# A decoder layer with the residual kept unscaled, one GpSimd instruction a norm, GpSimd's subtractions in quarters and a later load of x

## The chip, the cores and the metric

The kernel runs on one core of one Trainium2 chip. The metric is the device time of one execution in microseconds (us), the median of several runs. The engines that matter are TensorE (PE: matmuls, with its weight loads as PEld), VectorE (DVE), ScalarE (ACT), GpSimd (POOL), and the queue of SyncE (SP) that issues nearly all transfers.

## The reference

One decoder layer over 512 positions with 1024 features, all in 32-bit floats:

```
x = layer_norm(ALPHA * x + 0.5 * swiglu(x, ffn1...), ln1)        # first FFN, inner width 2816
q, f, i, g, conv_val, conv_gate = split(x @ w_in)
o_a = rms_norm(gated linear recurrence of q, f, i) * gain * sigmoid(g)      # 4 heads of 128
o_b = silu(layer_norm(causal conv of width 31 of conv_val * sigmoid(conv_gate)))
x = layer_norm(ALPHA * x + concat(o_a, o_b) @ w_out, ln2)
x = layer_norm(ALPHA * x + 0.5 * swiglu(x, ffn2...), ln3)        # second FFN
```

Here swiglu(x) is (silu(x @ w_gate) * (x @ w_up)) @ w_down, ALPHA is the fourth root of 2, layer_norm subtracts the mean, multiplies with (variance + epsilon) to the power of -1/2, and applies gain and bias. Multiplying the whole input of a layer norm by a constant changes nothing if its epsilon is multiplied by the constant's square.

## The kernel before

Every float32 product is made of three matmuls over operands that are split in two parts: `hi` is a rounded copy (`cast`, on ACT), and `lo` is what is left (`rest`, a subtraction raw - hi, L71). For weights the subtraction is on DVE or, for 22 units of 128x1024 that the middle part of the layer uses, on POOL (`plan(..., nc.gpsimd)`). The names in the trace are `raw` for loaded weights, `whi` and `wlo` for their parts, `h`, `hp`, `ah`, `al`, `xh`, `xl` for activations and their parts, `bank` for PSUM banks.

The order of the program is: a start, in which x and the first weights are loaded and split; the first FFN's gate and up products, in which most pairs of blocks use seven products in place of eight (L405); its down product in `rows_out`; the mix (projections by `cols` and `rows`, the recurrence's `scores`, the convolution on DVE at L759, its norm); the output projection, in `rows_out` again; and the second FFN like the first. TensorE's order is written out by hand (`manual_schedule`), and the instructions of the other engines are put in order by the framework's scheduler; each engine works through its own in that order. A weight load can start when a buffer of `raw` is free, a cast when one of six slots for parts is.

The residual stream lies in four tiles `xres`, one for each 128 positions. `rows_out` computes its product in two halves of 512 features. After the second half of tile i it does the following on DVE and POOL:

- `add` (L328, L329): xres = product * factor + xres on DVE, and the half's statistics.
- `norm` (L334 to L342): the statistics are joined (L334); `rstd_of` computes (variance * scale + epsilon) to the power of -1/2 with two POOL instructions of one element a partition (L216, L217); meanwhile DVE does (xres - mean) * gain in two halves (L338); then, once `rstd` is there, xres * rstd + bias in two halves (L342).
- `finish(i)`, later in PE's order: PE transposes the normed tile (L269 after the first FFN, L283 after the mix), ACT and DVE split the transposed tile (L272, L273; L285 to L287), and POOL multiplies the tile by ALPHA for the next residual sum (`scaled`, L292). After the second FFN the tile is stored instead.

So that PE has work while a tile is being normed, `follow` puts the first products of the next stage between the transposes of the last tiles, by the fixed counts in `NORM_WAITS`.

`scaled` is also called for x itself: `load_rest` (L638) loads the four tiles of x into `xres` and scales them; the text of the program calls it in the first FFN, ahead of its third pair of blocks. `rstd_of` also serves the convolution's norm (L865, one element a partition, four times) and the recurrence's norm (8 elements, twice).

Of the kernel before, what the change touches and what calls it, by code (L numbers as in the profile page):

```python
# [9 lines left out]
F32 = mybir.dt.float32  # L10
# [43 lines left out]
def decoder_layer(ctx, tc, x_tok, x_q, w_first, vec, bcast, ng, w_gu1, w_d1, w_i, w_g, w_col, w_o, w_gu2, w_d2, out):  # L54
# [13 lines left out]
        nc.scalar.copy(hi, raw)  # L68

    def rest(lo, raw, hi, engine=nc.vector):  # L70
        engine.tensor_tensor(lo, raw, hi.bitcast(F32), op=ALU.subtract)  # L71

    def split(raw, hi, lo, lo_engine):
        cast(hi, raw)
# [136 lines left out]
        for j in range(2):  # L211
            nc.sync.dma_start(out=t[:, j, :], in_=bcast[2 * i + j:2 * i + j + 1, :].broadcast_to([P, D]))

    def rstd_of(square, scale, eps, n):
        r = small.tile([P, n], F32, tag=f"rstd{n}", name="rstd")
        nc.gpsimd.tensor_scalar(r, square, scale, eps, op0=ALU.mult, op1=ALU.add)  # L216
        nc.gpsimd.tensor_tensor(r, r, negh.broadcast_to([P, n]) if n > 1 else negh, op=ALU.pow)  # L217
        return r

# [68 lines left out]
        if i == NT - 1:  # L288
            x.sums()

    def scaled(i):
        nc.gpsimd.tensor_scalar(xres[i], xres[i], ALPHA, 1.0, op0=ALU.mult, op1=ALU.mult)  # L292


    def run(steps):
        for _ in steps:
# [14 lines left out]
    def rows_out(ks, per, lhs, accs, factor, late, finish, follow=(), before=lambda u: None, then=lambda: None):  # L311

        n_units = len(ks) // per
        stats = [small.tile([P, 2, 6], F32, tag="stats", name="stats") for _ in range(NT)]

        def part(acc, u, hi, lo, i):
            for j in range(per):  # L320
                n = per * u + j
                h, l = lhs(ks[n])
                mm3(acc[i], h[:, i * P:(i + 1) * P], l[:, i * P:(i + 1) * P],
                    hi[:, j, :], lo[:, j, :], n == 0, n == len(ks) - 1)

        def add(acc, half, i):
            z = xres[i][:, half * 512:(half + 1) * 512]
            nc.vector.scalar_tensor_tensor(z, acc[i], factor, z, op0=ALU.mult, op1=ALU.add)  # L328
            nc.vector.bn_stats(stats[i][:, half, :], z)  # L329

        def norm(i):
            gain, bias = gb
            mv = small.tile([P, 2], F32, tag="mv", name="mv")
            nc.vector.bn_aggr(mv, stats[i])  # L334
            r = rstd_of(mv[:, 1:2], 1.0, LN_EPS, 1)
            for c in range(2):
                s = slice(c * 512, (c + 1) * 512)
                nc.vector.scalar_tensor_tensor(xres[i][:, s], xres[i][:, s], mv[:, 0:1], gain[:, s],  # L338
                                               op0=ALU.subtract, op1=ALU.mult)
            for c in range(2):  # L340
                s = slice(c * 512, (c + 1) * 512)
                nc.vector.scalar_tensor_tensor(xres[i][:, s], xres[i][:, s], r, bias[:, s],  # L342
                                               op0=ALU.mult, op1=ALU.add)

        acc = [bank(b) for b in accs[0]]
        with tc.manual_schedule(engines={PE}):
            for u in range(n_units):
                before(u)
                hi, lo = unit()
                for i in range(NT):  # L350
                    part(acc, u, hi, lo, i)
        for i in range(NT):
            add(acc, 0, i)
        acc = [bank(b) for b in accs[1]]
        for u in range(n_units - late):
            hi, lo = unit()
            for i in range(NT):
                part(acc, u, hi, lo, i)
        then()
        ahead(late)  # L360
        kept = [(u, *unit_now()) for u in range(n_units - late, n_units)]
        ahead(SLOTS - late)
        with tc.manual_schedule(engines={PE}):
            left = deque()
            for i in range(NT):
                for n, (u, hi, lo) in enumerate(kept):
                    part(acc, u, hi, lo, i)
                    if n == 0 and i >= 2 and left:
                        left.popleft()()
                if i == NT - 1:  # L370
                    ahead(SLOTS)
                add(acc, 1, i)
                norm(i)
                left.append(finish(i))
            follow = iter(follow)
            for wait in NORM_WAITS:
                while wait > 0.0 and (t := next(follow, None)) is not None:
                    wait -= t
                left.popleft()()
            run(follow)  # L380

    def four_halved(pp, banks):

        ahead(4)
        us = [unit_now() for _ in range(4)]
        xh, xl = operand
        pp.extend(bank(b) for b in banks)
        for t in range(2):
            sl = slice(256 * t, 256 * (t + 1))
            for ps, (hi, lo) in zip(pp, us):  # L390
                for k in range(NK):
                    mm3(ps[:, sl], hi[:, k, :], lo[:, k, :], xh[:, k, sl], xl[:, k, sl], k == 0, k == NK - 1)
                    yield MM3 / 2
        ahead(AHEAD)
# [70 lines left out]
                    yield MM3 / 2  # L465
        ahead(AHEAD)

    def ffn(x, begun, meanwhile, gb_i, finish, follow=(), then=lambda: None, later=lambda: None):
        with tc.tile_pool(name="ffn", bufs=1) as fp:

            slots = ["h2", "h3", "v", "c", "h4", "h5"]
# [31 lines left out]
            with tc.manual_schedule(engines={PE}):  # L503
                plain_gate_up(begun)
                for f in range(1, PLAIN):
                    ahead(4)
                    ws = [unit_now() for _ in range(2)]
                    ahead(3)
                    got = [bank(i, 2, H) for i in chain(*zip(*PAIR_BANKS[f % 2]))]
                    run(plain(got, x, ws))  # L510
                    plain_gate_up(got)
                for f in range(PLAIN, NP):
                    if f == PLAIN:
                        meanwhile()
                    h.append(h_of(f))
                    for s in range(2):
                        ahead(3)
                        w = unit_now()
                        ahead(3)
                        pr = Pair(PAIR_BANKS[f % 2][s], work_tile() if s else h[f])  # L520
                        for n in USUAL:
                            run(pr.steps(x, w, (n,)))
                            if f == PLAIN and s == 0 and n == "p7":
                                x.last_sum()
                        gate_up(s, pr)
# [35 lines left out]
                f, l = divmod(n, 2)  # L561
                return tuple(y[:, l * T:(l + 1) * T] for y in hp[f])

            rows_out(range(NF), 2, lhs, FFN_ACCS, 0.5, 4, finish, follow, before, then)


    x1 = Halves()
# [67 lines left out]
            nc.gpsimd.tensor_copy(masks[:, n, :], mf)  # L635
        nc.gpsimd.tensor_copy(masks[:, len(MASKED), :], ident)

    def load_rest():  # L638
        for i in range(NT):
            nc.sync.dma_start(out=xres[i], in_=x_tok[i])  # L640
            scaled(i)

    def after(transpose, b):
        def finish(i):
            def rest():
                transpose(i, b)
                scaled(i)
            return rest
        return finish

    def lazily(make, *args):
# [4 lines left out]
    def next_operand(make):  # L656
        operand[:] = make()

    ffn(x1, begun, load_rest, 0, after(transposed, 4), four_halved(conv_first, (6, 7, 0, 1)),
        lambda: next_operand(plain_operand), make_masks)  # L660
    xh, xl = operand


    with tc.tile_pool(name="mix", bufs=1) as mp:
# [162 lines left out]
        def values(hp):  # L827
            for h in range(2):
                ps = bank(nbank[h][0], NT, P)
                for i in range(NT):  # L830
                    for j in range(i + 1):
                        s = diag[h][:, i, :] if i == j else off[h][:, at[j, i] * P:(at[j, i] + 1) * P]
                        nc.tensor.matmul(ps[:, i, :], lhsT=s, rhs=v[:, j, (2 * hp + h) * P:(2 * hp + h + 1) * P],  # L833
                                         start=(j == 0), stop=(j == i))
                nc.scalar.copy(ot[:, :, 2 * hp + h, :], ps)
                sq = small.tile([P, NT, P], F32, tag="work", name="sq", bufs=2)
                nc.scalar.activation(sq, ps, AF.Square)
                nc.vector.tensor_reduce(ss[:, 2 * hp + h, :], sq, axis=mybir.AxisListType.X, op=ALU.add)

        def norm_gate(hp, b):  # L840

            r = rstd_of(ss[:, 2 * hp:2 * hp + 2, :].rearrange("p a b -> p (a b)"), 1.0 / P, RMS_EPS, 2 * NT)
            for h in range(2):
                n = 2 * hp + h
                for i in range(NT):
# [9 lines left out]
        def conv_norm():  # L855

            def forth(i):
# [4 lines left out]
                nc.vector.bn_stats(stt, ps.rearrange("p a b -> p (a b)"))  # L862
                mv = small.tile([P, 2], F32, tag="mv", name="mv")
                nc.vector.bn_aggr(mv, stt)
                r = rstd_of(mv[:, 1:2], 1.0, LN_EPS, 1)  # L865
                cn = small.tile([P, 4, P], F32, tag="work", name="cn", bufs=2)
                nc.vector.tensor_scalar(cn, ps, mv[:, 0:1], r, op0=ALU.subtract, op1=ALU.mult)
                return cn
# [58 lines left out]
        def gates_between(u):  # L927
# [3 lines left out]
            elif u == 3:  # L931
# [2 lines left out]
        begun = []  # L934
        rows_out((4, 5, 6, 7, 0, 1, 2, 3), 2,
                 lambda k: (ah[:, k, :], al[k]) if k < NH else (bh[:, k - NH, :], bl[k - NH]),
                 ((2, 3, 6, 7), (0, 1, 4, 5)), 1.0, 4, after(transposed_halves, 6),
                 lazily(lambda: begin(begun, operand[0], (2, 3, 0, 1))),
                 before=gates_between, then=lambda: next_operand(lambda: [Halves()]))

# [3 lines left out]
            nc.sync.dma_start(out=out[i * P:(i + 1) * P, s], in_=xres[i][:, s])  # L944
        return lambda: None

    ffn(operand[0], begun, lambda: None, 2, store)


# [58 lines left out]
```

## Time and profile before

| | |
|---|---|
| time, median of 3 runs | 946.73 us (946.48 to 947.9) |
| the profiled execution, its own time | 949.64 us |
| its span from first to last instruction | 947.9 us |
| busy: PE, DVE, ACT, POOL | 932.6, 692.7, 388.6, 132.3 us |
| transfers | 96.67 MB, 102 GB/s in the mean |

The span is some 1.7 us shorter than the execution's own time, and this execution took 2.9 us longer than the median. Busy time is the time in which an engine works on an instruction; PE's matmuls overlap, and their ends are modelled, so its busy time holds some time in which it waits for its pipeline.

### The profile page before, as it was taken

The page shows a single profiled execution, that of the slowest core. Times are in us where ns is not written, and L with a number is a line of the kernel's source. Part 1 is how long each engine was busy: PE and PEld are TensorE (multiplying, and loading weights), DVE is VectorE, ACT ScalarE, POOL GpSimd, SP SyncE. Part 2 cuts the span into 40 slices and gives each one's busy share as a digit, 9 for nine tenths or more (in the row PEclk, how much of TensorE's full clock was granted, in tenths as well). Part 3 has the DMA queues.
Part 4 walks back from the last instruction along what each step waited for, and adds up shares of the span by engine and source line. Part 5 has one row for each costly group of instructions (what it writes and reads, how often), then busy time and mean ns, then how long its engine had stood idle before and what let it go on. Part 6 is the DMA issues. An engine that isn't in the chain of part 4 may idle for free.

```text
span 947.9 us, 14234 instructions
## 1 busy us (share of the span) xinstructions
PE 932.6 (98%) x5913; PEld 843.8 (89%) x5913; DVE 692.7 (73%) x915; ACT 388.6 (41%) x560; POOL 132.3 (14%) x106
## 2 busy tenths in 40 slices
PE   9999999999999999999999999999999999999996
PEld 6799999999888889888888888989999999988885
DVE  6988888887624276999887658958888888742417
ACT  5554555556421123414341723534555545722100
POOL 1100000000910035532352204100000000000002
PEclk9999999999999999999999999999999999999998
DMA  8432322324423303321130251223223222452302
GB/s 295 155 131 90 134 90 97 127 68 145 156 89 92 108 22 101 124 88 45 51 123 5 63 166 44 87 85 123 101 92 132 90 90 90 133 156 90 99 13 89
DMA packets 22464, 96.67 MB, mean 102 GB/s; under 512 B 2496, under 2 KB 3648, under 8 KB 17024
## 3 DMA queue, kind: packets, MB, share of 16 engines
q1 hardware_dynamic: 22320, 95.50, 30.1%
q8 instruction: 46, 0.75, 0.3%
q0 software_dynamic: 80, 0.26, 0.1%
q14 instruction: 18, 0.15, 0.1%
HBM read 93.66 MB, written 2.10 MB: 101 GB/s over the span
## 4 chain that ended last, share of the span: by engine, by line
PE 48%; DVE 3%; POOL 1%; issue 0%; POOLq 0%; DVEq 0%; ACT 0%
PE bank L405 19%; PE bank L191 9%; PE bank L189 9%; PE bank L190 9%; PE bank L776 1%; PE bank L833 1%; DVE wlo L71 1%; DVE xres L342 0%; POOL rstd L217 0%; DVE al L286 0%; PE bank L799 0%; POOL rstd L216 0%; DVE qk L808 0%; DVE diag L816 0%; DVE stats L329 0%
## 5 line engine op out<-in xcount | busy, mean ns | idle before, releaser
L71 DVE TENSOR_TENSOR wlo<-raw,whi 128x1024 fp32r<-128x1024 f32 (+2 forms) x150 | 175.1, 1175 | 146.6 <-ACT whi L68 146.5
L68 ACT CAST whi<-raw 128x1024 fp32r<-128x1024 f32 (+2 forms) x172 | 173.4, 1013 | 254.8 <-PE bank L191 151.8
L189 PE MATMUL bank<-whi,hp 128*128 128x512 f32 x320 | 124.7, 390 | 0.0
L191 PE MATMUL bank<-whi,hp 128*128 128x512 f32 x320 | 124.5, 389 | 0.0
L190 PE MATMUL bank<-wlo,hp 128*128 128x512 f32 x320 | 124.5, 389 | 0.0
L405 PE MATMUL bank<-ah,whi 128*128 128x256 f32 x432 | 122.3, 283 | 0.0
L405 PE MATMUL bank<-bh,whi 128*128 128x256 f32 x432 | 122.3, 283 | 0.0
L405 PE MATMUL bank<-bl,whi 128*128 128x256 f32 x432 | 122.3, 283 | 0.0
L405 PE MATMUL bank<-ah,wlo 128*128 128x256 f32 x432 | 122.2, 283 | 0.0
L405 PE MATMUL bank<-al,whi 128*128 128x256 f32 x432 | 122.2, 283 | 0.0
L405 PE MATMUL bank<-bh,wlo 128*128 128x256 f32 x432 | 122.1, 283 | 0.0
L405 PEld LDWEIGHTS bank<-bh,whi 128*128 128x128 f32 x432 | 82.9, 192 | 0.0
L405 PEld LDWEIGHTS bank<-bl,whi 128*128 128x128 f32 x432 | 82.9, 192 | 0.0
L405 PEld LDWEIGHTS bank<-bh,wlo 128*128 128x128 f32 x432 | 82.9, 192 | 0.0
L405 PEld LDWEIGHTS bank<-al,whi 128*128 128x128 f32 x432 | 82.9, 192 | 0.1
L405 PEld LDWEIGHTS bank<-ah,whi 128*128 128x128 f32 x432 | 82.8, 192 | 0.1
L405 PEld LDWEIGHTS bank<-ah,wlo 128*128 128x128 f32 x432 | 82.8, 192 | 0.0
L759 DVE SCALAR_TENSOR_TENSOR bank<-u,vecs,bank 128x512 f32<-128x512 f32 x120 | 81.2, 751 | 1.8 <-ACT bank L754 1.6
L216 POOL TENSOR_SCALAR rstd<-mv 128x1 f32<-128x1 f32 x16 | 8.7, 542 | 466.9 <-DVE mv L334 451.7
L191 PEld LDWEIGHTS bank<-whi,hp 128*128 128x128 f32 x320 | 60.1, 188 | 12.5
L190 PEld LDWEIGHTS bank<-wlo,hp 128*128 128x128 f32 x320 | 60.1, 188 | 12.5
L189 PEld LDWEIGHTS bank<-whi,hp 128*128 128x128 f32 x320 | 60.1, 188 | 12.2
(193 smaller groups left out, 1963.1 us busy)
## 6 DMA issues: line engine op xcount, KB each, us to landing
raw<-w_gu SPq DMA_DIRECT2D x42, 1024.0 KB, 4.8
raw<-w_d SPq DMA_DIRECT2D x44, 512.0 KB, 3.5
raw<-w_col SPq DMA_DIRECT2D x16, 512.0 KB, 3.5
raw<-w_o SPq DMA_DIRECT2D x8, 512.0 KB, 3.4
xres<-x_tok SPq DMA_DIRECT2D x4, 512.0 KB, 7.8
gb<-bcast SPq DMA_DIRECT2D x4, 512.0 KB, 4.7
raw<-w_i SPq DMA_DIRECT2D x4, 512.0 KB, 3.4
raw<-w_g SPq DMA_DIRECT2D x4, 512.0 KB, 3.4
```

The source lines that it names most:

```text
L68: nc.scalar.copy(hi, raw)
L71: engine.tensor_tensor(lo, raw, hi.bitcast(F32), op=ALU.subtract)
L189: nc.tensor.matmul(ps, lhsT=lh, rhs=rh, start=first, stop=False)
L190: nc.tensor.matmul(ps, lhsT=lh, rhs=rl, start=False, stop=False)
L191: nc.tensor.matmul(ps, lhsT=ll, rhs=rh, start=False, stop=last)
L216: nc.gpsimd.tensor_scalar(r, square, scale, eps, op0=ALU.mult, op1=ALU.add)
L405: nc.tensor.matmul(ps, lhsT=l[:, k, :], rhs=r[:, k, :], start=first and k == 0 and j == 0, stop=k == 3 and j == 2, skip_group_check=True)
L759: nc.vector.scalar_tensor_tensor(accs[n], us[n][:, j:j + T], vecs[:, w:w + 1], accs[n], op0=ALU.mult, op1=ALU.add)
L776: nc.tensor.matmul(ps[:, g, :], lhsT=k[:, h, sl], rhs=q[:, h, sl], start=True, stop=True)
L833: nc.tensor.matmul(ps[:, i, :], lhsT=s, rhs=v[:, j, (2 * hp + h) * P:(2 * hp + h + 1) * P], start=(j == 0), stop=(j == i))
```

## The change

- `xres` holds the normed tile itself and not ALPHA times it. The products are added with the factor divided by ALPHA (0.5 / ALPHA or 1 / ALPHA), and the norms over this sum use epsilon / ALPHA squared. The 12 POOL instructions of `scaled` (128x1024 each) are gone.
- `rstd_of` has one POOL instruction: the epsilon is added by a DVE instruction, and the recurrence's mean over 128 features is made by a scale in ACT's squaring, which was there before. There are 18 such norms.
- A subtraction on POOL is issued as four instructions of a quarter of the columns (128x256). Those on DVE stay whole.
- The text of the program loads x later: after `make_masks`, in the first FFN's down product.

```diff
     def rest(lo, raw, hi, engine=nc.vector):
-        engine.tensor_tensor(lo, raw, hi.bitcast(F32), op=ALU.subtract)
+
+        n = raw.shape[-1]
+        step = n // 4 if engine is nc.gpsimd else n
+        for j in range(0, n, step):
+            sl = slice(j, j + step)
+            engine.tensor_tensor(lo[..., sl], raw[..., sl], hi.bitcast(F32)[..., sl], op=ALU.subtract)
...
-    def rstd_of(square, scale, eps, n):
+    def rstd_of(square, eps, n):
         r = small.tile([P, n], F32, tag=f"rstd{n}", name="rstd")
-        nc.gpsimd.tensor_scalar(r, square, scale, eps, op0=ALU.mult, op1=ALU.add)
+        nc.vector.tensor_scalar(r, square, eps, None, op0=ALU.add)
         nc.gpsimd.tensor_tensor(r, r, negh.broadcast_to([P, n]) if n > 1 else negh, op=ALU.pow)
...
-    def scaled(i):
-        nc.gpsimd.tensor_scalar(xres[i], xres[i], ALPHA, 1.0, op0=ALU.mult, op1=ALU.mult)
...
-            r = rstd_of(mv[:, 1:2], 1.0, LN_EPS, 1)
+            r = rstd_of(mv[:, 1:2], LN_EPS / ALPHA ** 2, 1)
...
-                    if f == PLAIN:
-                        meanwhile()
...
-            rows_out(range(NF), 2, lhs, FFN_ACCS, 0.5, 4, finish, follow, before, then)
+            rows_out(range(NF), 2, lhs, FFN_ACCS, 0.5 / ALPHA, 4, finish, follow, before, then)
...
-    def load_rest():
+    def later():
+        make_masks()
         for i in range(NT):
             nc.sync.dma_start(out=xres[i], in_=x_tok[i])
-            scaled(i)
...
-            def rest():
-                transpose(i, b)
-                scaled(i)
-            return rest
+            return lambda: transpose(i, b)
...
-                nc.scalar.activation(sq, ps, AF.Square)
+                nc.scalar.activation(sq, ps, AF.Square, scale=P ** -0.5)
```

The first place is SyncE's queue near the start of the program. These are its rows before; `vec` is a small table, `x_tok` is x by tiles, `w_gu` the first FFN's weights and `w_d` those of its down product:

```order
L603 DMA vecs<-vec 128x144
L640 DMA xres_73<-x_tok 128x1024
L640 DMA xres_74<-x_tok 128x1024
L98 DMA raw<-w_gu 128x2048 x2
L640 DMA xres_75<-x_tok 128x1024
L640 DMA xres_76<-x_tok 128x1024
L98 DMA raw<-w_gu 128x2048 x18
```

And these are the same rows of the change:

```order
L603 DMA vecs<-vec 128x144
L641 DMA xres_73<-x_tok 128x1024
L641 DMA xres_74<-x_tok 128x1024
L103 DMA raw<-w_gu 128x2048 x2
L641 DMA xres_75<-x_tok 128x1024
L641 DMA xres_76<-x_tok 128x1024
L103 DMA raw<-w_gu 128x2048 x18
```

Nothing moved: the scheduler had put x's four loads there before, and it does so still.

The second place is POOL from the last tile's norm after the first FFN to the recurrence's first norm. Before (`u` is the convolution's input, `ss` the recurrence's sums of squares):

```order
L217 TENSOR_TENSOR rstd<-rstd,negh 128x1
L71 TENSOR_TENSOR wlo<-raw,whi 128x1024 x2
L740 MEMSET u 128x30 x4
L292 TENSOR_SCALAR xres_76<-xres_76 128x1024
L71 TENSOR_TENSOR wlo<-raw,whi 128x1024 x16
L216 TENSOR_SCALAR rstd<-ss 128x8
L217 TENSOR_TENSOR rstd<-rstd,negh 128x8
L71 TENSOR_TENSOR wlo<-raw,whi 128x1024 x4
```

With the change:

```order
L222 TENSOR_TENSOR rstd<-rstd,negh 128x1 x4
L76 TENSOR_TENSOR wlo<-raw,whi 128x256 x8
L737 MEMSET u 128x30 x4
L76 TENSOR_TENSOR wlo<-raw,whi 128x256 x76
L222 TENSOR_TENSOR rstd<-rstd,negh 128x8
L76 TENSOR_TENSOR wlo<-raw,whi 128x256 x4
```

The 22 subtractions became 88, the scaling is gone, and the recurrence's first power now stands behind 21 of the 22 units, where it stood behind 18.

The third place is DVE at the last norm of the program. Before:

```order
L328 SCALAR_TENSOR_TENSOR xres_76<-bank_8223,xres_76 128x512
L329 BN_STATS stats<-xres_76 128x6
L334 BN_AGGR mv<-stats 128x2
L338 SCALAR_TENSOR_TENSOR xres_76<-xres_76,mv,gb 128x512 x2
L342 SCALAR_TENSOR_TENSOR xres_76<-xres_76,rstd,gb 128x512 x2
```

With the change:

```order
L330 SCALAR_TENSOR_TENSOR xres_76<-bank_8277,xres_76 128x512
L331 BN_STATS stats<-xres_76 128x6
L336 BN_AGGR mv<-stats 128x2
L221 TENSOR_SCALAR rstd<-mv 128x1
L340 SCALAR_TENSOR_TENSOR xres_76<-xres_76,mv,gb 128x512 x2
L344 SCALAR_TENSOR_TENSOR xres_76<-xres_76,rstd,gb 128x512 x2
```

The epsilon's addition stands between the joined statistics and the first of the long instructions; so it does in each of the 18 norms. Apart from these 18 rows DVE's order is unchanged, and PE's is unchanged throughout.

## Rows read from the trace of the kernel before

**Rows 1.** PE's waits over the whole span: total us, times, longest.

```profile
PE bank L269 <- DVE xres L342: 2.0, 1, 2.0
...
PE bank L283 <- DVE xres L342: 1.2, 1, 1.2
PE bank L795 <- DVE m L808: 0.8, 1, 0.8
PE bank L191 <- DVE wlo L71: 0.6, 1, 0.6
PE bank L776 <- DVE qk L808: 0.5, 2, 0.4
PE bank L190 <- DVE al L286: 0.4, 1, 0.4
```

**Rows 2.** Timeline of PE, 27 to 29 us (start, length, instruction, idle before).

```profile
27.17 0.40 PE L189 MATMUL bank<-ah,whi 128*128 128x512 f32 x1
27.41 0.40 PE L190 MATMUL bank<-al,whi 128*128 128x512 f32 x1
28.42 0.50 PE L191 MATMUL bank<-ah,wlo 128*128 128x512 f32 x1 [0.61 <-DVE wlo L71]
```

**Rows 3.** Timeline of POOL and DVE in the start.

```profile
18.01 3.54 POOL L292 TENSOR_SCALAR xres<-xres 128x1024 f32<-128x1024 f32 x2 [16.29 <-DMA xres<-x_tok]
...
20.55 1.01 DVE L608 TENSOR_TENSOR mx<-vecs 128x4 f32<-128x4 f32 x1
...
34.53 0.15 DVE L609 TENSOR_TENSOR e<-vecs,mx 128x4 f32<-128x4 f32 x1
```

**Rows 4.** Timeline of POOL and DVE, norm after the first FFN, last tile.

```profile
361.55 5.19 POOL L71 TENSOR_TENSOR wlo<-raw,whi 128x1024 fp32r<-128x1024 f32 x2 [0.82 <-ACT whi L68]
...
361.61 2.90 DVE L342 SCALAR_TENSOR_TENSOR xres<-xres,rstd,gb 128x512 f32<-128x512 f32 x1
...
361.61 5.67 DVE L342 SCALAR_TENSOR_TENSOR xres<-xres,rstd,gb 128x512 f32<-128x512 f32 x2
```

**Rows 5.** Timeline of POOL and DVE in the first scores, 438 to 444 us.

```profile
439.21 2.38 POOL L71 TENSOR_TENSOR wlo<-raw,whi 128x1024 fp32r<-128x1024 f32 x1 [6.66 <-ACT whi L68]
...
439.33 2.28 DVE L812 TENSOR_TENSOR totals<-totals 128x8 f32<-128x8 f32 x1
```

**Rows 6.** Timeline of DVE and POOL, norm after the mix.

```profile
578.50 2.20 DVE L342 SCALAR_TENSOR_TENSOR xres<-xres,rstd,m 128x512 f32<-128x512 f32 x2 [0.44 <-POOL rstd L217]
...
585.36 2.20 DVE L342 SCALAR_TENSOR_TENSOR xres<-xres,rstd,m 128x512 f32<-128x512 f32 x2 [0.44 <-POOL rstd L217]
...
585.41 1.62 POOL L292 TENSOR_SCALAR xres<-xres 128x1024 f32<-128x1024 f32 x1
```

**Rows 7.** Timeline of DVE and POOL, last norm of the program.

```profile
941.12 0.21 DVE L334 BATCH_NORM_AGGREGATE mv<-stats 128x2 f32<-128x12 f32 x1
941.36 1.42 DVE L338 SCALAR_TENSOR_TENSOR xres<-xres,mv,gb 128x512 f32<-128x512 f32 x2
943.22 1.42 DVE L342 SCALAR_TENSOR_TENSOR xres<-xres,rstd,gb 128x512 f32<-128x512 f32 x2 [0.44 <-POOL rstd L217]
...
941.41 0.75 POOL L216 TENSOR_SCALAR rstd<-mv 128x1 f32<-128x1 f32 x1 [3.67 <-DVE mv L334]
942.25 0.94 POOL L217 TENSOR_TENSOR rstd<-rstd,negh 128x1 f32<-128x1 f32 x1
```

**Rows 8.** Timeline of DVE and POOL: a small addition, and a power beside L338.

```profile
35.63 0.17 DVE L615 TENSOR_SCALAR oml<-lb 128x4 f32<-128x4 f32 x1
...
360.18 0.55 POOL L217 TENSOR_TENSOR rstd<-rstd,negh 128x1 f32<-128x1 f32 x1
...
360.29 1.41 DVE L338 SCALAR_TENSOR_TENSOR xres<-xres,mv,gb 128x512 f32<-128x512 f32 x2
```

**Rows 9.** Timeline of POOL, and groups by form: busy us, mean ns, idle before.

```profile
501.46 1.27 POOL L719 TENSOR_TENSOR m<-m,ngb 128x512 f32<-128x512 f32 x1 [6.40 <-ACT m L718]
...
L71 POOL TENSOR_TENSOR wlo<-raw,whi 128x1024 fp32r<-128x1024 f32 x22 | 53.1, 2418 | 76.8 <-ACT whi L68 76.8
```

More of the change, by code (lines that the diff above doesn't have):

```diff
@@ L466, in begin, with ffn @@
         ahead(AHEAD)
-    def ffn(x, begun, meanwhile, gb_i, finish, follow=(), then=lambda: None, later=lambda: None):
+    def ffn(x, begun, gb_i, finish, follow=(), then=lambda: None, later=lambda: None):
         with tc.tile_pool(name="ffn", bufs=1) as fp:
@@ L657, in next_operand @@
         operand[:] = make()
-    ffn(x1, begun, load_rest, 0, after(transposed, 4), four_halved(conv_first, (6, 7, 0, 1)),
-        lambda: next_operand(plain_operand), make_masks)
+    ffn(x1, begun, 0, after(transposed, 4), four_halved(conv_first, (6, 7, 0, 1)),
+        lambda: next_operand(plain_operand), later)
     xh, xl = operand
@@ L836, in values @@
                 sq = small.tile([P, NT, P], F32, tag="work", name="sq", bufs=2)
-                nc.scalar.activation(sq, ps, AF.Square)
+                nc.scalar.activation(sq, ps, AF.Square, scale=P ** -0.5)
                 nc.vector.tensor_reduce(ss[:, 2 * hp + h, :], sq, axis=mybir.AxisListType.X, op=ALU.add)
         def norm_gate(hp, b):
-            r = rstd_of(ss[:, 2 * hp:2 * hp + 2, :].rearrange("p a b -> p (a b)"), 1.0 / P, RMS_EPS, 2 * NT)
+            r = rstd_of(ss[:, 2 * hp:2 * hp + 2, :].rearrange("p a b -> p (a b)"), RMS_EPS, 2 * NT)
             for h in range(2):
@@ L864, in forth @@
                 nc.vector.bn_aggr(mv, stt)
-                r = rstd_of(mv[:, 1:2], 1.0, LN_EPS, 1)
+                r = rstd_of(mv[:, 1:2], LN_EPS, 1)
                 cn = small.tile([P, 4, P], F32, tag="work", name="cn", bufs=2)
@@ L936, in decoder_layer @@
                  lambda k: (ah[:, k, :], al[k]) if k < NH else (bh[:, k - NH, :], bl[k - NH]),
-                 ((2, 3, 6, 7), (0, 1, 4, 5)), 1.0, 4, after(transposed_halves, 6),
+                 ((2, 3, 6, 7), (0, 1, 4, 5)), 1.0 / ALPHA, 4, after(transposed_halves, 6),
                  lazily(lambda: begin(begun, operand[0], (2, 3, 0, 1))),
@@ L945, in store @@
         return lambda: None
-    ffn(operand[0], begun, lambda: None, 2, store)
+    ffn(operand[0], begun, 2, store)
 def kernel(**inputs):
```

## Prediction

> **What bounds the kernel.** I first read PE's own waits, because everything else matters only through them. The view lists a handful, each a place where PE stood for another engine [rows 1]: 2.0 us for the normed tile after the first FFN (L342), 1.2 us for the normed tile after the mix, 0.8 us for the scores' product on DVE (L808), 0.6 us for a weight's `wlo` in the start, 0.4 us for a transposed tile's `al` (L286), and 0.5 us in two pieces for `qk` in the second scores. The reader is to see that all of them end with DVE, and that their sum, 5.5 us, is nearly all that this change can reach before the program's tail, where PE is done and the last norm and its store run alone.
>
> The waits are a little longer than the view says, since it counts from the end of the matmul before, and matmuls overlap. One matmul starts 0.24 us after the other (27.17, 27.41) though each lasts 0.40 [rows 2]; the late one starts 1.01 after its predecessor, so that 0.77 us are lost where the view says 0.61. I add 0.16 us to each wait.
>
> Then I asked why DVE was late at each place, with the timelines of DVE and POOL beside each other. At four of them a DVE instruction with two tensors in SBUF stands still while POOL works on SBUF:
> - Start: POOL scales two tiles of x (L292) from 18.01 to 21.55. DVE's L608, four elements, takes 1.01 us there; a like one at 34.53 takes 0.15 [rows 3].
> - Norm after the first FFN: POOL subtracts two units from 361.55 to 366.74. DVE's L342, two halves, takes 5.67 us [rows 4] where the last norm's takes 1.42 [rows 7]. The first half ends at 361.61 + 2.90 = 364.51, with POOL's pair still running: DVE got in between two POOL instructions, and POOL's pair took 5.19 where two alone are 4.84, twice the mean of 2.42 [rows 9].
> - First scores: POOL's unit from 439.21 to 441.59, and DVE's L812, eight elements, takes 2.28 us and ends with it [rows 5].
> - Norm after the mix: beside POOL's L292, L342 takes 2.20 us twice [rows 6], 0.78 more than 1.42.
>
> So POOL holds DVE for the length of one POOL instruction at a time, and the change shortens or removes just those.
>
> **The change, part by part.**
>
> *Scaling removed.* 12 POOL instructions go. In the start L608 comes out 1.01 - 0.15 = 0.86 us earlier, and that alone covers the 0.77 lost at 28.42: gain 0.77, if the cast of the weights in front of the late `wlo` is not kept by its transfer, and 0 if it is. I take 0.77. In the norm after the mix, DVE gains 0.78 at 585.36 (and as much at 578.50, part of which PE's own pace takes back). `al` follows next on DVE, 0.4 + 0.16 = 0.56 late: gain 0.56.
>
> *One POOL instruction a norm.* Before, the last norm runs: statistics end at 941.33, L338 ends at 942.78, `rstd` at 943.19, L342 starts at 943.22 [rows 7]. DVE waits 0.44 us for POOL. Now the addition goes first. The nearest row is a DVE instruction on four elements, 0.17 us [rows 8]; with a step of 0.03 as between 941.33 and 941.36, L338 runs from 941.56 to 942.98. POOL's power starts with it and took 0.94 us beside L338 before [rows 7], so it ends near 942.55, under the cover of L338. L342 follows L338 at 942.9: 0.3 us earlier. From below, were the power as late behind L338 as before (943.19 - 942.78 = 0.41), L342 would start at 943.4, 0.2 us later than before. I take the gain of 0.3, since the power alone is 0.55 us [rows 8] and needs only to fit beside 1.42. In the program's tail that is 0.3 us on the path. In the norm after the mix the last two tiles' norms give 0.3 each and, with 0.78, 1.38 us: just what the transposes there were late (1.2 + 0.16 = 1.36), before the other 0.78 is counted: gain 1.36. In the recurrence's and convolution's norms, nothing on DVE hides the addition, but a POOL instruction of about the same length and a handover go in turn: 0, with 0.1 either way at each of the two waits for `qk`, so the 0.5 us stays.
>
> [...]
>
> *Quarters.* 22 instructions become 88. No row has 128x256 on POOL. Between 128x512 (1.27 us, another operation) and 128x1024 (2.42) [rows 9] each 512 columns cost 1.15; a quarter is then about 0.70 us and a unit 2.8. The bounds are a fourth of a unit, 0.60, and the 1.27 itself; I take 0.70, on the line between. The added 0.4 us a unit costs nothing while POOL waits: over its 22 units it stood 76.8 us for ACT's casts [rows 9], 3.5 us a unit; without that cover weights would come late (below). In the norm after the first FFN each half of L342 now waits for at most a quarter, so the pair ends by 361.61 + 2 x (0.70 + 0.71) = 364.4 and not 367.28. That is 2.8 us earlier where 2.0 + 0.16 = 2.16 are lost: gain 2.16. In the scores, L812 ends within 0.70 + 0.15 = 0.85 us and not 2.28, 1.4 earlier where 0.8 + 0.16 = 0.96 are lost: gain 0.96. The recurrence's first power stands three units further back, in a stretch where POOL waits for work; 0.
>
> *x loaded later.* The order of the queue shows the four loads of x at the same place, so this part does nothing: 0. The new constants are immediates of instructions that were there: 0.
>
> Sum: 0.77 + 0.56 + 1.36 + 0.3 + 2.16 + 0.96 = 6.1 us. The profiled execution took 949.64 us (span 947.9), so a like one would take 943.5; it is 2.9 above the median of 946.73, and from that the forecast is **940.6 us**.
>
> **The rivals.**
> [...]
> - *The norm after the mix stays late*: DVE's gain there goes into waits for ACT's casts, whose slots PE frees at its own pace, and 0.56 + 1.36 are not won: 942.5. The fit of 1.38 to 1.36 is tight; the second 0.78 speaks against it.
> [...]
> - *Slower: POOL becomes the bound.* If a quarter costs much more than 0.70, because each start or each turn with DVE is dear, POOL falls behind in the mix. It had 53.1 + 76.8 = 129.9 us for its 22 units [rows 9], 1.48 us a quarter; that is where it decides. At 1.6 us, 88 quarters are 140.8, PE would wait 10.9 us for weights, and the time would be 951.5. The bound of 1.27 lies under the point.
>
> **How the numbers follow.** The forecast has 0.6, the power 0.15, the norm after the mix 0.12, the ports kept 0.08, POOL as the bound 0.03, and 0.02 something unseen. About 0.2%, 1.9 us, is what a measurement of this kernel can tell from no change. The first three cases are faster by more, with most of the unseen at neither end: faster 0.88, same 0.08, slower 0.04. The range goes up to 943.6, past the first three cases and with some half of the gain in the norm after the first FFN (1.1) lost besides; the ports kept and POOL as the bound stay outside. Down it goes to 939.2: the 0.5 + 0.32 of `qk` won as well, and the spread of the runs before, 946.48 to 946.73 and more.
>
> **What would show it.** Right: no PE wait over 0.3 us at L269, L283, L795, L286 and the start's `wlo`; L342 beside POOL at most 1.5 us a half, and never 2.8; quarters of 0.6 to 0.8 us; DVE's wait for `rstd` in the layer norms gone and the last L342 starting 0.3 us sooner after its statistics; x's transfers at the same times. Wrong: quarters over 1 us; L342 of the last tile after the first FFN still ending with POOL's last quarter; PE waits for `wlo` in the mix; a new wait of DVE for ACT's casts between 580 and 600 us.

## The result, and the profile after

The changed kernel takes **942.60 us** (median of 5 runs, 942.41 to 943.09). The kernel before, in the same comparison, takes 946.73 us (5 runs, 946.20 to 947.90). The ratio is 0.9944 with an interval of 0.9928 to 0.9960. It is 4.1 us faster; the forecast was 940.6 us, 6.1 us faster, with a range of 939.2 to 943.6.

The profiled execution took 942.62 us with a span of 940.6. I read PE's waits first, as for the kernel before (total us, times, longest):

```profile
PE bank L578 <- DVE idle L575: 1.3, 1, 1.3
PE bank L773 <- DVE qk L805: 0.3, 1, 0.3
```

The first row belongs to the idle matmuls at the very start, and stood in the kernel before too. All five waits of [rows 1] that the prediction wanted to remove are gone; of its sixth, for `qk`, one piece is left. (Lines have moved: L76 is now the subtraction, L222 the power, L340 and L344 are the two long steps of a norm, L805 and L809 the scores' products.)

At the last tile's norm after the first FFN, where [rows 4] had 5.67 us, the timelines of POOL and of DVE now show this; the first POOL row is cut out of the second by a narrower window:

```profile
360.92 1.19 POOL L76 TENSOR_TENSOR wlo<-raw,whi 128x256 fp32r<-128x256 f32 x1
...
360.09 6.20 POOL L76 TENSOR_TENSOR wlo<-raw,whi 128x256 fp32r<-128x256 f32 x8 [0.64 <-ACT whi L68]
...
359.62 1.89 DVE L344 SCALAR_TENSOR_TENSOR xres<-xres,rstd,gb 128x512 f32<-128x512 f32 x2
```

The pair takes 1.89 us where an undisturbed one takes 1.41: it lost 0.48 us. POOL's quarter at 360.92 took 1.19 where an undisturbed one takes 0.73: it lost 0.46. DVE had started first here. The two engines took turns at the border of an instruction, as the 2.90 in [rows 4] had suggested.

In the first scores (POOL, then DVE), to be held against [rows 5]:

```profile
435.96 2.81 POOL L76 TENSOR_TENSOR wlo<-raw,whi 128x256 fp32r<-128x256 f32 x4 [5.25 <-ACT whi L68]
...
435.81 0.15 DVE L809 TENSOR_TENSOR totals<-totals 128x8 f32<-128x8 f32 x1
...
438.07 1.78 DVE L805 TENSOR_TENSOR m<-m,totals 128x1024 f32<-128x1024 f32 x1
```

A unit of four quarters takes 2.81 us, as estimated (2.8). The small product L809 now starts just ahead of the unit and takes 0.15; the product behind it takes 1.78 instead of 1.21, so that 0.57 us are lost to a quarter where 2.13 were lost to a whole unit. PE does not wait for it.

In the norm after the mix [rows 6], beside which POOL now has only the power, DVE shows:

```profile
580.04 1.41 DVE L344 SCALAR_TENSOR_TENSOR xres<-xres,rstd,m 128x512 f32<-128x512 f32 x2
...
591.11 1.41 DVE L344 SCALAR_TENSOR_TENSOR xres<-xres,rstd,m 128x512 f32<-128x512 f32 x2
```

And the last norm of the program [rows 7], DVE and then POOL:

```profile
934.28 0.21 DVE L336 BATCH_NORM_AGGREGATE mv<-stats 128x2 f32<-128x12 f32 x1
934.52 0.15 DVE L221 TENSOR_SCALAR rstd<-mv 128x1 f32<-128x1 f32 x1
934.59 1.41 DVE L340 SCALAR_TENSOR_TENSOR xres<-xres,mv,gb 128x512 f32<-128x512 f32 x2
935.91 1.41 DVE L344 SCALAR_TENSOR_TENSOR xres<-xres,rstd,gb 128x512 f32<-128x512 f32 x2
...
934.82 0.92 POOL L222 TENSOR_TENSOR rstd<-rstd,negh 128x1 f32<-128x1 f32 x1 [4.52 <-DVE rstd L221]
```

L344 has no wait any more. It starts 1.42 us after the joined statistics (934.28 + 0.21 = 934.49, to 935.91); before it was 1.89 (941.33 to 943.22). The power ran from 934.82 to 935.74, wholly beside L340's pair, which took its usual 1.41. It was POOL that lost time there: 0.92 us, where a power with no DVE instruction beside it takes 0.55 (the convolution's four norms of this kernel).

In the start [rows 3], where POOL has no scaling any more, DVE's small L608 shows:

```profile
20.68 0.16 DVE L608 TENSOR_TENSOR mx<-vecs 128x4 f32<-128x4 f32 x1
```

### The profile page after: what moved, and what is told of

It is laid out like the page before. It is cut to its first block, busy times and chain, and to the rows that moved or that the text cites. A ratio compares the mean times of both kernels' runs of the same rounds, so it can differ in the third digit from the quotient of the medians.

```text
span 940.6 us, 14283 instructions
## 1 busy us (share of the span) xinstructions
PE 931.2 (99%) x5913; PEld 844.0 (90%) x5913; DVE 679.8 (72%) x933; ACT 388.2 (41%) x560; POOL 119.3 (13%) x142
## 4 chain that ended last, share of the span: by engine, by line
PE 98%; DVE 2%; POOL 0%; issue 0%; DVEq 0%; ACT 0%
PE bank L407 39%; PE bank L196 18%; PE bank L194 18%; PE bank L195 18%; PE bank L773 2%; PE bank L830 1%; PE bank L578 0%; PE bank L796 0%; PE bank L288 0%; PE bank L274 0%; DVE qk L805 0%; DVE diag L813 0%; PE bank L792 0%; PE bank L847 0%; DVE cn L864 0%
## 5 line engine op out<-in xcount | busy, mean ns | idle before, releaser
L76 DVE TENSOR_TENSOR wlo<-raw,whi 128x1024 fp32r<-128x1024 f32 (+2 forms) x150 | 173.5, 1163 | 148.2 <-ACT whi L68 148.1
L222 POOL TENSOR_TENSOR rstd<-rstd,negh 128x1 f32<-128x1 f32 (+1 forms) x18 | 17.9, 997 | 497.4 <-DVE rstd L221 497.4
L76 POOL TENSOR_TENSOR wlo<-raw,whi 128x256 fp32r<-128x256 f32 x88 | 66.5, 789 | 63.3 <-ACT whi L68 61.4
L196 PEld LDWEIGHTS bank<-whi,hp 128*128 128x128 f32 x320 | 60.1, 188 | 12.4
```

Source lines behind the costliest of these rows:

```text
L76: engine.tensor_tensor(lo[..., sl], raw[..., sl], hi.bitcast(F32)[..., sl], op=ALU.subtract)
L196: nc.tensor.matmul(ps, lhsT=ll, rhs=rh, start=False, stop=last)
```

## The experiments

Theory P is the prediction's: POOL holds DVE for the length of one POOL instruction at a time, as in [rows 4] and [rows 5], and each part of the change removes the waits that it was given. Rival N puts the gain in the norms and not in the pieces. Theory V came with the result: the profiled execution of before was 2.9 us above its median, so one of its waits may belong to that execution and not to the kernel; by P it would come back in another execution. e1 to e4 ran beside the kernel before on one chip (its median there 947.44 us), e5 to e8 in a second comparison (947.49), e9 to e11 in a third (948.03).

**e1: the kernel before once more.** No edit.

> The kernel before, unchanged, once more. [...]

Measured: 947.26 us (946.27 to 951.80, 12 runs). Its profiled execution has these waits of PE:

```profile
PE bank L283 <- DVE xres L342: 1.2, 1, 1.2
PE bank L795 <- DVE m L808: 0.8, 1, 0.8
PE bank L191 <- DVE wlo L71: 0.6, 1, 0.6
PE bank L190 <- DVE xl L273: 0.5, 1, 0.5
PE bank L776 <- DVE qk L808: 0.5, 2, 0.4
```

The largest wait of [rows 1], 2.0 us at L269, is not there. The timelines of POOL, DVE and ACT at that place say why:

```profile
363.19 5.25 POOL L71 TENSOR_TENSOR wlo<-raw,whi 128x1024 fp32r<-128x1024 f32 x2 [1.65 <-ACT whi L68]
...
362.42 1.41 DVE L342 SCALAR_TENSOR_TENSOR xres<-xres,rstd,gb 128x512 f32<-128x512 f32 x2
...
362.06 1.05 ACT L68 CAST whi<-raw 128x1024 fp32r<-128x1024 f32 x1 [2.79 <-DMA raw<-w_col]
```

In [rows 4] POOL's first unit started at 361.55, 0.06 us ahead of L342, and held it. Here the weight landed later, its cast began at 362.06, POOL's unit at 363.19, and L342 had started 0.77 us before: 1.41, no hold. It is a race between a weight's transfer and a norm, and the norm wins or loses it from one execution to the next. The kernel loses when the weight comes early enough for POOL to start first. V holds.

**e2: quarters alone** in the kernel before.

```diff
-        engine.tensor_tensor(lo, raw, hi.bitcast(F32), op=ALU.subtract)
+        n = raw.shape[-1]
+        step = n // 4 if engine is nc.gpsimd else n
+        for j in range(0, n, step):
+            sl = slice(j, j + step)
+            engine.tensor_tensor(lo[..., sl], raw[..., sl], hi.bitcast(F32)[..., sl], op=ALU.subtract)
```

> The kernel before, with the subtractions on POOL in quarters and nothing else. Theory P: PE's waits at L269 (2.0) and L795 (0.8) go, those of the start (0.6), L190 (0.4) and L283 (1.2) stay: 946.7 - 3.1 = 943.6. Rival N (the gain comes from the shorter way through POOL in each norm, which all waits for L342 have in common): the waits for L342 stay, 946.5.

Measured: 946.44 us (945.82 to 946.89, 12 runs), ratio 0.9980 (0.9968 to 0.9991): 1.0 us faster, and not 3.1. PE's wait for the scores is gone and the other waits stay (1.2 at the transposes after the mix, 0.6 in the start, 0.5 for `qk`, 0.3 for `al`). The 1.0 us are near the scores' term, 0.96. L269 has no wait here either, with L342's successor at 1.90 us beside eight quarters; DVE had started first. The highest of the twelve runs is 0.5 us above their median, while eight of the 31 runs of the kernel before beside them lie at 949.4 to 952.2, 1.9 us and more above theirs: no run with the quarters alone lies so high.

**e3: unscaled residual alone**: `scaled` removed, factors and epsilon divided, `load_rest` as in the changed kernel.

```diff
-            r = rstd_of(mv[:, 1:2], 1.0, LN_EPS, 1)
+            r = rstd_of(mv[:, 1:2], 1.0, LN_EPS / ALPHA ** 2, 1)
...
-                scaled(i)
...
-            rows_out(range(NF), 2, lhs, FFN_ACCS, 0.5, 4, finish, follow, before, then)
+            rows_out(range(NF), 2, lhs, FFN_ACCS, 0.5 / ALPHA, 4, finish, follow, before, then)
```

> The kernel before without the scaling (divided factors and epsilons), with the two POOL instructions a norm and with whole subtractions. Theory P: the wait of the start and those at L190 and most of that at L283 go (0.77 + 0.56 + 0.8 to 1.36), L269 and L795 stay: 944.0 to 944.6. Rival N: only the start's wait changes, 946.0.

Measured: 944.00 us (943.95 to 945.70, 9 runs), ratio 0.9961 (0.9948 to 0.9974): 3.4 us faster. Only these two waits of PE for DVE are left beside the idle one:

```profile
PE bank L787 <- DVE m L800: 0.8, 1, 0.8
PE bank L768 <- DVE qk L800: 0.5, 2, 0.4
```

The start's, both waits of the norm after the mix, and e1's `xl` went together. At the norm after the first FFN the two engines were nearly level, POOL 0.15 us behind:

```profile
360.45 5.66 POOL L71 TENSOR_TENSOR wlo<-raw,whi 128x1024 fp32r<-128x1024 f32 x2 [1.03 <-ACT whi L68]
...
360.30 3.56 DVE L339 SCALAR_TENSOR_TENSOR xres<-xres,rstd,gb 128x512 f32<-128x512 f32 x2
```

The first half ran, the second was held for one unit, and PE had the room for that.

**e4: one-instruction norm alone.**

```diff
-        nc.gpsimd.tensor_scalar(r, square, scale, eps, op0=ALU.mult, op1=ALU.add)
+        nc.vector.tensor_scalar(r, square, eps, None, op0=ALU.add)
```

> The kernel before with the epsilon added on DVE and one POOL instruction a norm, and nothing else. Theory P: DVE's wait for rstd of 0.44 us goes in the norms, worth 0.3 us in the tail and some 0.3 at L283; all other waits of PE stay: 946.1. Rival N: the waits of PE for L342 (2.0 and 1.2) go, 943.2 or less.

Measured: 945.13 us (944.69 to 947.36, 11 runs), ratio 0.9972 (0.9960 to 0.9983): 2.3 us faster, between the two expectations and met by neither. PE's waits:

```profile
PE bank L795 <- DVE m L808: 0.8, 1, 0.8
PE bank L283 <- DVE xres L342: 0.5, 1, 0.5
PE bank L776 <- DVE qk L808: 0.3, 1, 0.3
```

The norm after the mix is 0.7 us less late (0.5 and not 1.2) though the scaling still stands beside it. So the norm's edit and the scaling's edit pay for the same wait: the scaling's edit alone takes all of it, the norm's alone about half, and their gains do not add up. The sum of the three parts alone, 1.0 + 3.4 + 2.3 = 6.7, is more than the 4.1 to 4.7 that all of them bring together; each of the three has an interval of some 1.1 us either way, so it is the lists of waits that show the overlap, more than this sum. The start's wait is not listed in this execution, though nothing of this edit touches the start. PE's timeline there:

```profile
27.67 0.39 PE L190 MATMUL bank<-al,whi 128*128 128x512 f32 x1
28.20 0.50 PE L191 MATMUL bank<-ah,wlo 128*128 128x512 f32 x1
```

The second matmul starts 0.53 us after the first, where [rows 2] had 1.01: the wait is shorter by 0.5 us and not gone. What moved it I did not find out.

**e5: the changed kernel with whole subtractions** (e2's edit taken back).

> The changed kernel with its subtractions on GpSimd whole again; the unscaled residual and the one-instruction norm stay. Theory P (POOL holds DVE for the length of one of its instructions): the scores' wait comes back, 0.8 to 1.0 us on PE, and nothing else, since at the norm after the first FFN L344's first half starts 0.5 us before POOL's unit (359.62 and 360.09 in the changed kernel) and only its second half is held, with PE not late: 1.0 us above the changed kernel run beside it, about 943.6. Rival (the waits add up over the parts, and the quarters were worth the 2.16 + 0.96 of the prediction): 3.1 us above it, about 945.7.

Measured: 944.02 us (943.42 to 944.94, 7 runs), against 942.76 for the changed kernel beside it (e6): quarters are worth 1.3 us there, near P's 1.0 and far from 3.1. The seven times are two groups:

```
943.42 943.43 943.69 944.02    944.80 944.89 944.94
```

The profiled execution is the one of 944.89. Its waits of PE, and its POOL and DVE rows at the norm after the first FFN:

```profile
PE bank L269 <- DVE xres L339: 1.1, 1, 1.1
PE bank L787 <- DVE m L800: 0.8, 1, 0.8
```

```profile
359.57 5.34 POOL L71 TENSOR_TENSOR wlo<-raw,whi 128x1024 fp32r<-128x1024 f32 x2
...
359.77 5.69 DVE L339 SCALAR_TENSOR_TENSOR xres<-xres,rstd,gb 128x512 f32<-128x512 f32 x2
```

This is the race once more, lost by 0.20 us: 5.69, and 5.67 in [rows 4]. So my expectation that L344 would win it in this kernel was wrong. The two groups of times, some 1.3 us apart, fit V's two kinds of execution (1.1 + 0.16 for the wait); the lower group was not profiled in this kernel. In five of the six profiles with whole units and no added delay the order of the starts is seen to decide: POOL first in the first profile, in e5 and in e9 (the pair takes 5.67 to 5.69, PE waits 1.1 to 2.0); POOL 0.15 us behind in e3 (3.56, no wait); POOL 0.77 us behind in e1 (1.41, no wait). The sixth, e4, has no wait there either.

**e6: the changed kernel once more.** No edit.

> The changed kernel unchanged, on the same chip as the parts: 942.4 to 943.1, with the same two PE waits as in its first profile. The kernel before had some runs 2 to 5 us above its median; if those are the runs in which POOL starts ahead of L342 at the norm after the first FFN, none of these runs lies more than 1.5 us above its median. If the tail of slow runs has another cause, about one in four of these runs does too.

Measured: 942.76 us (942.70 to 943.40, 6 runs), the same two waits of PE. The highest run is 0.6 us above the median. Of the kernel before, 18 of the 63 runs in the three comparisons lie between 949.1 and 952.2 us, the medians being 947.4 to 948.0; of e1's twelve runs one does. The changed kernel has no run more than 0.7 us above its median in 11, and e2 none in 12; of e3's nine, with whole units, one lies 1.7 us above. The 13 highest of the 63, from 949.9 up, are more than the wait of 2.0 + 0.16 can add to 947.4. In nine of these 13 the mean granted clock of the run is 0.995 or 0.996; in the 50 runs below it is 0.997 or 0.998 throughout.

**e7 and e8: DVE delayed at that norm**, in the kernel before and in the changed kernel. The two added instructions write a tile that nobody reads.

```diff
+            if i == NT - 1 and not delayed:
+                delayed.append(small.tile([P, 2, 6], F32, tag="extra", name="extra", bufs=1))
+                for c in range(2):
+                    nc.vector.bn_stats(delayed[0][:, c, :], xres[i][:, 0:512])
             for c in range(2):
                 s = slice(c * 512, (c + 1) * 512)
                 nc.vector.scalar_tensor_tensor(xres[i][:, s], xres[i][:, s], r, bias[:, s],
```

> The kernel before with two more DVE instructions (statistics of 512 columns whose result nobody reads, about 1.4 us together) between L338 and L342 of the last tile's norm after the first FFN, so that POOL's two units always start ahead of L342. Theory P: L342 is then held through both units in every run, ends some 5 us after POOL starts, and PE waits there 2.2 to 2.9 us: 949.6 to 950.3, in all runs. Rival (PE was late there for another reason, and the tile has the room): the 1.4 us vanish in the about 2.2 us that PE leaves, and the time is that of the kernel before, 947.4.

> The changed kernel with the same two DVE instructions at the same place. Theory P: each half of L344 waits for at most one quarter, so the pair takes at most 2.9 us and ends about 363.9 where PE comes to it: 0 to 0.3 us over the changed kernel, 942.6 to 942.9, no PE wait over 0.3 there. [...]

Measured: e7 954.18 us (951.91 to 955.44, 6 runs); e8 944.64 us (944.41 to 945.19, 9 runs). By the times alone both missed: e7 is 4 us above P's figure, and e8 1.7 us above. The traces say which part is whose. First e7: PE's wait, POOL and DVE there, and then windows of PE (us, busy time with instructions, granted clock, DMA share, GB/s):

```profile
PE bank L269 <- DVE xres L348: 3.3, 1, 3.3
...
363.63 5.15 POOL L71 TENSOR_TENSOR wlo<-raw,whi 128x1024 fp32r<-128x1024 f32 x2 [1.71 <-ACT whi L68]
...
364.01 5.32 DVE L348 SCALAR_TENSOR_TENSOR xres<-xres,rstd,gb 128x512 f32<-128x512 f32 x2
```

```profile
364.00:366.00 2.00, 2.00 (x19) 1.00 0.00 0
366.00:369.00 3.00, 0.17 (x2) 1.00 0.50 175
369.00:370.00 1.00, 0.53 (x5) 1.00 0.31 37
370.00:371.00 1.00, 1.00 (x10) 0.85 0.73 246
371.00:372.00 1.00, 1.00 (x6) 0.50 0.62 250
...
370.00:375.00 5.00, 5.00 (x32) 0.66 0.27 99
375.00:380.00 5.00, 5.00 (x44) 1.00 0.01 3
```

POOL started 0.38 us ahead and the pair took 5.32. PE waits 3.3 us, a little more than P's 2.2 to 2.9. It works on at first at a granted clock of 1.00, and then for about 3 us at 0.50: 6 matmuls in a microsecond. The windows from 370 to 375 hold 32 matmuls where the next five microseconds hold 44; the 12 that are missing, at 0.12 us each, as matmuls of 256 columns start in the first profile (372.08, 372.20), are 1.4 us. So a wait of 3.3 us costs 3.3 + 0.16 + 1.4 = 4.9. The wait of 2.0 in the first profile was followed by no lower clock; the same windows there:

```profile
367.40:369.00 1.60, 1.57 (x14) 1.00 0.66 179
369.00:371.00 2.00, 2.00 (x19) 1.00 0.31 123
```

In e8 the trace has no wait of PE at L269. POOL and DVE there:

```profile
360.18 6.67 POOL L76 TENSOR_TENSOR wlo<-raw,whi 128x256 fp32r<-128x256 f32 x8
...
361.58 1.89 DVE L350 SCALAR_TENSOR_TENSOR xres<-xres,rstd,gb 128x512 f32<-128x512 f32 x2
```

POOL started 1.4 us ahead and the pair still took only 1.89: its halves got in between the quarters. That POOL holds DVE through all its quarters once it has started first is out at this place. The 1.9 us by which e8 is above e6 arise elsewhere. Most 512-column matmuls start 0.226 or 0.227 us after the one before, and some 0.229 to 0.240 (at one place 282.28 and 282.51 in e6, 282.67 and 282.91 in e8). Counted in the traces over all neighbouring pairs, e6 has 213 of the longer kind and e8 500; what they take beyond 0.227 sums to 1.2 and 2.9 us, so that e8 pays 1.7 us more. The added ones lie in the two down products, from 260 to 360 us and from 840 us on, so before the norm and long after it. e7 has 507, against 218 in e1, and pays 1.6 us more. What the delay has to do with this I don't know: the edit brings two instructions and a tile, and no run has the one without the other. It is in both kernels, and drops out of the comparison between them: 954.18 - 944.64 = 9.5 us, where the kernels without the delay differ by 4.7; the further 4.8 are, to 0.1, the 4.9 of the wait with its lower clock.

**e9: the scalings after the norms moved to ACT**, in the kernel before; the four of the start stay on POOL.

```diff
+    def scaled_act(i):
+        nc.scalar.activation(xres[i], xres[i], AF.Copy, scale=ALPHA)
...
                 transpose(i, b)
-                scaled(i)
+                scaled_act(i)
```

> The kernel before, with the eight scalings that follow the norms done by ACT and not by POOL (the four of the start stay on POOL). Theory P (what cost was POOL's hold on DVE, not the scaling as such): L342 beside them falls from 2.20 to 1.4 us; at the norm after the mix the al wait goes and L283's 1.39 + 0.2 shrinks to 0.6 or less; the start's and the scores' waits stay: 1.2 to 2.0 us under the kernel before, 945.4 to 946.2. Rival (the work itself is in the way, wherever it is done, for instance because ACT then comes late with its casts): within 0.5 us of the kernel before, 946.9 to 947.9.

Measured: 945.63 us (945.01 to 947.72, 12 runs), ratio 0.9975 (0.9966 to 0.9985). The time is in P's range and not in the rival's; against the kernel before beside it the gain is 2.4 us, where P had 1.2 to 2.0. Seven runs lie at 945.0 to 945.7, five at 946.6 to 947.7. DVE and ACT in the norm after the mix, where the tile is scaled as before but by another engine:

```profile
585.05 1.42 DVE L345 SCALAR_TENSOR_TENSOR xres<-xres,rstd,m 128x512 f32<-128x512 f32 x2 [0.44 <-POOL rstd L217]
...
584.81 1.07 ACT L295 ACTIVATE xres<-xres 128x1024 f32<-128x1024 f32 x1
```

2.20 became 1.42 beside the same work [rows 6]: what cost was POOL's hold and not the scaling. The transposes' wait after the mix is not in the list any more; the start's 0.6 and the scores' 0.8 are, as P said. Beside ACT's scaling of 1.07 DVE's pair took 1.42, as in [rows 7]; ACT's four scalings after the mix take 1.06 to 1.07. The profiled execution is the slowest run, 947.72, and has the wait at L269 (1.5 us).

**e10 and e11: halves and eighths** in the changed kernel; the edit of e10 is shown, e11 has n // 8.

```diff
-        step = n // 4 if engine is nc.gpsimd else n
+        step = n // 2 if engine is nc.gpsimd else n
```

> The changed kernel with its subtractions on GpSimd in halves, not quarters. Theory P: the hold is one half, 1.2 to 1.3 us; the scores' product had about 1.2 us of room before PE waited (2.13 us lost, 0.94 waited), so it gains or loses 0 to 0.2 there, and L344 after the first FFN loses at most 2.5 us in the runs in which POOL starts first, PE waiting 0 to 0.5: 942.7 to 943.2 beside 942.7 of quarters. Rival (a piece must be as short as the DVE instruction it stands beside): both waits come back in half, 943.5 or more.

> The changed kernel with its subtractions on GpSimd in eighths. Theory P: 176 instructions of about 0.42 us (from 0.70 a quarter and 2.42 a whole: 0.57 us for 256 columns and 0.13 fixed), a unit 3.3 us, POOL's total 74 us; POOL still waits for ACT's casts, no new PE wait: within 0.3 us of the changed kernel, 942.4 to 943.0. Rival (POOL as the bound): the fixed part is larger, a unit takes over 5 us, weights come late in the mix and PE waits for wlo: 945 or more.

Measured: halves 942.46 us (942.34 to 943.18), eighths 942.47 us (942.40 to 943.10), 5 runs each; neither can be told from quarters (942.60 and 942.76). Halves are a little under P's range, eighths inside it. Neither has a PE wait that quarters have not. In the first scores of e10 POOL's halves started 0.26 us ahead of DVE's small product, which was held as P says:

```profile
436.11 1.03 DVE L809 TENSOR_TENSOR totals<-totals 128x8 f32<-128x8 f32 x1
```

It took 1.03 us where it takes 0.15 undisturbed, and PE was not late. At the norm after the first FFN DVE started first in this profile, so that a hold by halves is not seen there. POOL's groups by form in the changed kernel, e10 and e11 (busy us, mean ns, idle before):

```profile
L76 POOL TENSOR_TENSOR wlo<-raw,whi 128x256 fp32r<-128x256 f32 x88 | 66.5, 789 | 63.3 <-ACT whi L68 61.4 <-PE bank L195 1.8
```

```profile
L76 POOL TENSOR_TENSOR wlo<-raw,whi 128x512 fp32r<-128x512 f32 x44 | 56.3, 1304 | 72.8 <-ACT whi L68 70.5 <-PE bank L830 2.4
```

```profile
L76 POOL TENSOR_TENSOR wlo<-raw,whi 128x128 fp32r<-128x128 f32 x176 | 79.6, 489 | 50.5 <-ACT whi L68 50.3
```

Whole units took 53.1 us [rows 9], so each halving adds 3 to 13 us of POOL's time, waits for DVE included, and POOL still waits 50.5 us for casts at eighths. As far as these runs show, all that was needed is that a piece be no longer than DVE's room, and a half (1.3 us) already is.

## Why the prediction was right, and where its size was off

Direction, mechanism and range held; the gain was 4.1 to 4.7 us (942.60 against 946.73, and 942.76 against 947.49) and not 6.1. The range held although one term of the sum was worth almost nothing to the median, because its upper end allowed for the loss of half of that term and for the rivals besides; that part is luck. By its own steps:

- *Norm after the first FFN, 2.16: the step that failed.* The mechanism is right (e1, e5, e7 and e8 show hold and cure), the size is not. The prediction read the wait from an execution of 949.64 us, took the gain off, and then also took off that execution's 2.9 us above the median, of which this very wait was 2.2. e1's profile has no such wait, and 45 of the 63 later runs lie below 948.6, so the kernel mostly runs without it and its removal moves the median by little: the median of those 45 is 947.4, that of all 63 947.5. e2 measured quarters at 1.0 us and not 3.1. When the race is lost, the wait was 1.1 to 2.0 us (e5, e9, [rows 1]). Without this term the sum is 3.95, and 946.73 - 3.95 = 942.8.
- *Start, 0.77.* In the changed kernel L608 takes 0.16 us (1.01 in [rows 3]), and PE has no wait there; gone in e3, still there in e2. Right, with the reservation of e4, where the wait shrank by 0.5 without this edit.
- *Norm after the mix, 0.56 + 1.36.* Both waits are gone, as forecast, and the rival that they stay is out: that its 942.5 lies next to the measured time is chance. But the 1.36 was put down to the norm's 0.3 a tile and the scaling's 0.78 together, as if both were needed: e3 shows that the scaling's removal alone does it, e4 that the norm alone does half. In e1 no wait for `al` is listed, but one of 0.5 for `xl` (L273), in the norm after the first FFN, behind an L342 of 2.21 us beside POOL's scaling: the same kind of hold.
- *Tail, 0.3.* It is 0.47 (1.89 to 1.42): the forecast let L340 wait 0.2 us for the addition, but it starts 0.07 us after the addition has started (934.52, 934.59).
- *Scores, 0.96.* e2 measured 1.0, and e5 1.3 with some of its runs lengthened by the race. The way was not quite the forecast's: with quarters the small product started 0.15 us ahead of POOL and was not held at all, and the long product behind it lost 0.57. That a shortened hold does not reach PE either is what e10 shows.
- *A quarter, 0.70, a unit 2.8.* The undisturbed unit shown above took 2.81.
- *x loaded later, 0.* The loads are issued at 11.8 and 20.0 us, and before at 11.2 and 19.1.
- *The rivals.* The chance of 0.15 for the power: no run shows that it holds DVE. In the tail DVE's two halves take their 1.41 beside it, and it is the power that takes 0.92 and not 0.55; in [rows 8], where the power began 0.11 us ahead, the pair took 1.41 too. What a long POOL instruction does, DVE's pair shows in e5: 5.69 us beside two whole units. The chance of 0.08 for the ports kept: no run shows ports, and none shows quarters that hold DVE one after the other; in e8 the pair took 1.89 us beside eight quarters that had begun 1.4 us ahead. POOL is not the bound, not even at 176 pieces (in e11 it waits 50.5 us).

## What to carry to other kernels

A profile is one execution: if it lies above the median, look for the wait that makes it so before you count the gain of removing it, and count it once. A wait that hangs on which of two engines starts first, by 0.06 us in [rows 4], came and went between executions here (2.0 us there, none in e1); removing it narrowed the spread (18 of 63 runs at 949.1 us and more before, none of 12 with the quarters alone; the whole change has 11 runs within 0.7 us) more than it moved the median. And two edits that shortened the same chain ahead of the same wait (the 1.2 us at L283, in e3 and e4) did not add up; run each alone and both together.

## What the runs showed of the hardware that was not expected

- Behind PE's wait of 3.3 us in e7 its granted clock was 0.50 for about 3 us, and the five microseconds around that time held 32 matmuls where the next five held 44; behind the wait of 2.0 us in the first profile it stayed at 1.00. The runs of before from 949.9 us up may be executions of that kind: nine of the 13 have a mean granted clock of 0.995 or 0.996, and e7's six have 0.994 to 0.997. None of the 13 was profiled.
- In the traces 512-column matmuls do not all start 0.227 us apart at the same granted clock of 1.00: some start 0.229 to 0.240 apart, and how many differs between programs with the same PE instructions (213 in e6, 500 in e8). The cause stays open.
- POOL and DVE took turns at the border of a POOL instruction: in e8 both halves of DVE's pair got in between quarters (1.89 us beside eight quarters, 1.4 us after they began), and in the changed kernel a quarter beside such a pair took 1.19 us instead of 0.73.
- Beside the power it was POOL that lost time: in the changed kernel's twelve layer norms the power takes 0.92 to 1.00 us beside L340's pair and the pair 1.41, and in the convolution's four norms, with no DVE instruction beside it, the power takes 0.55.
